# SP's transfers of a convolution loop in source order, and new start columns for the gate tiles of a ConvFFN

## The chip, the cores and the metric

The kernel runs on one core of a Trainium2 chip. The metric is the device time of one execution in microseconds (us). Engines: PE (TensorE matrix multiply; PEld is its weight load), DVE (VectorE), ACT (ScalarE), POOL (GpSimd) and SP (SyncE, which issues all the DMA transfers spoken of here).

## The reference

Two layers over 1024 latent tokens and 256 context tokens, model width 1024. Layer 0 mixes tokens with a Conformer convolution, layer 1 with windowed attention; each mixer is followed by a gated ConvFFN of inner width 2816, and each of these four steps is preceded by an RMSNorm with shift, scale and gate from an adaLN map of the conditioning vector. The two steps that the change touches (`dwconv` is a depthwise convolution, of 31 taps in the first and 3 in the second):

```python
def conformer_conv(h, w_pw1, b_pw1, w_dw, b_dw, ln_g, ln_b, w_pw2, b_pw2):
    u = h @ w_pw1 + b_pw1
    a, g = jnp.split(u, 2, axis=-1)
    v = a * jax.nn.sigmoid(g)
    v = dwconv(v, w_dw, b_dw)
    v = jax.nn.silu(layernorm(v, ln_g, ln_b))
    return v @ w_pw2 + b_pw2

def conv_ffn(h, w_up, w_dw, b_dw, w_down):
    u = dwconv(h @ w_up, w_dw, b_dw)
    a, b = jnp.split(u, 2, axis=-1)
    return (jax.nn.silu(a) * b) @ w_down
```

## The kernel before

**Layout.** Channels lie on the 128 partitions, tokens along the free axis, in three token tiles t = 0, 1, 2 of 512, 512 and 256 columns. Float32 products are made of three matrix products of rounded parts (`mm3`, matmuls at L193): each operand is split into a high part (`wh`, `x_h`, `gh`) and a remainder (`wl`, `x_l`, `gl`). Weights come by `load_raw` (L109) as 512 KB tiles `raw`, of which there are two buffers that all weights and adaLN blocks share; `split_pending` (L129, L131) makes `wh` and `wl`.

**Convolution loop (about 85 to 370 us).** It runs over 8 channel chunks c. A pass of c = 0 to 6 makes the next chunk's gated value v(c+1) with `glu_mm` (matmuls into `glu_ps`), `glu_gate` (ACT) and `glu_mul` (DVE), one token tile after the other, and convolves the chunk c: some taps on PE (`pe_taps`, `cacc`, L822), the others on DVE, ACT and POOL (`conv_steps`). PE needs shifted copies of v across partitions. So `Shifted.load(t)` stores piece t of v to DRAM (L799) and then reads it back with four `copy` transfers (L792), into `vp` for t = 0 and 1 and into `vpb` for t = 2. The copies wait until the store has landed, and that wait is SP's.

Each pass also makes one adaLN block 4 + c (`ada_steps`, matmuls into `ada_ps` at L211), of four parts of two matmuls with a 512 KB `raw` each. Parts 0 and 1 of the pass c have been fetched at the end of the pass c - 1 (`ld_ada(c, 0)` and `ld_ada(c, 1)`), parts 2 and 3 within the pass c (`ld_ada(c, 2)`, `ld_ada(c, 3)`), each after the part that frees its buffer. In the source a pass names, as far as SP is concerned:

```python
run(ada, 2)
...
ld_ada(c, 2)
ld_ada(c, 3)
...
vp.load(0)
...
w_load()
w_load()
...
vp.load(1)
...
ld_ada(c + 1, 0)
...
vp.load(2)
...
ld_ada(c + 1, 1)
```

(`run(ada, 2)` is parts 0 and 1 on PE; `w_load` fetches the next chunk's `pw1` weights.) The last pass, c = 7, has no next chunk: it convolves chunk 7 with 28 taps on PE, makes the last adaLN block, and calls `load_ada(0)` to `load_ada(3)` (L878), each a fetch of 2 MB for adaLN blocks of layer 1, which PE works on between the steps that follow the loop.

**Who orders the work.** The loop stands in a `tc.manual_schedule(engines=CONV_ENGINES)` block, in which PE, ACT, DVE and POOL issue in source order. SP is not among these engines: its order in the loop is the scheduler's, any order that the buffers and the data allow. The queue of an engine is in order, so what stands behind a waiting transfer on SP waits too.

**First ConvFFN (about 555 to 1490 us).** 22 channel groups j: two up projections (`up_ps`), three taps on ACT and DVE into a tile `c`, SiLU and product, and the split into `gh` and `gl` (`gate_steps`). After every second group the down projection (`down_half`, `down_mm`) multiplies `gh` and `gl` as moving operands by the down weights into `dn_ps`. `gh` and `gl` are tiles of the pool `fp` with three buffers each and W = 1024 + 2 + 256 = 1282 float32 columns, and a token tile is a slice of them at column 0, 512 or 1026. The last pair lies in halves of one older tile, `last_g`, whose first half starts where the tile does and the second W columns on; its products also feed `dn_tail`. The second ConvFFN has two token tiles (W = 1024) and its own pool.

Starts in the text are positions in a partition in bytes, mod 512, of a tile's first element; they follow from the order and the sizes of the tiles in the pools.

Of the kernel before, what the change touches and what calls it, by code (L numbers as in the profile page):

```python
# [8 lines left out]
F32 = mybir.dt.float32  # L9
# [9 lines left out]
P = 128  # L19
# [33 lines left out]
def hybrid_dit_kernel(  # L53
# [336 lines left out]
    def ffn(l, x_pool, fpool_stack, fpool, pas, pa, tiles, pieces, after_piece, on_half, cbufs, gbufs, extra=None, last_g=None):  # L390
        xs = list(x)
        W = SEQ + 2 + CTX if len(tiles) == 3 else SEQ
        pof = (0, 512, SEQ + 2)

        def up_ps(first=False):
# [31 lines left out]
            return c, [s0, s1, s2]  # L427

        def gate_steps(ca, cb, res, windows=((0, W),), g=None):
            gh, gl = g or [fpool.tile([P, W], F32R, tag=tag, name=tag, bufs=gbufs)  # L430
                           for tag in ("gh", "gl")]
            res.append((gh, gl))
            steps = []
            for o, e in windows:
                def s0(o=o, e=e):
                    nc.vector.tensor_mul(out=cb[:, o:e], in0=ca[:, o:e], in1=cb[:, o:e])

                def s1(o=o, e=e):
                    nc.scalar.copy(out=gh[:, o:e], in_=cb[:, o:e])
                    nc.vector.tensor_sub(out=gl[:, o:e], in0=cb[:, o:e], in1=gh[:, o:e])  # L440

                steps += [s0, s1]
            return steps
# [165 lines left out]
    with ExitStack() as cs:  # L609
# [250 lines left out]
        def ymean(c):  # L860
            for t, (o, n) in enumerate(TOK):
                nc.tensor.matmul(mean_ps[32 * t:32 * t + 32, :n], lhsT=ones2, rhs=ys[t][:, c, :],
                                 start=c == 0, stop=c == KC - 1)
# [41 lines left out]
        def ld_ada(c, u):  # L905
            if c < KC:
                araw[c, u] = load_raw(adaw[0, 4 + c, :, 2 * u:2 * u + 2, :])
# [14 lines left out]
        with tc.manual_schedule(engines=CONV_ENGINES):  # L922
            load_next(True)
            stats(0)
            ada0(2)
            bcast_a(0)
            bcast_b(0)
            normalize_h(0)
            ada0(0)
            load_next(True)  # L930
            load_block(1)
            load_h(2, nc.sync)
            w4 = load_taps()
            apply(0, 0, 2)
            stats(1, nc.vector, 0, 4)
            apply(0, 2, 4)
            split_pending()
            split_pending()
            q = glu_begin(0)
            ada0(3)  # L940
            stats(1, nc.vector, 4, 8)
            glu_mm(q, 0, 0, 0)
            stats(2, nc.vector, 0, 4)
            stats(2, nc.vector, 4, 8)
            bcast_a(1)
            ada0(1)
            bcast_a(2)
            bcast_b(1)
            apply(0, 4, 6)
            apply(0, 6, 8)  # L950
            glu_mm(q, 0, 1, 0)
            glu_mm(q, 0, 0, 1)
            normalize_h(1)
            glu_mm(q, 0, 1, 1)
            apply(1, 0, 2)
            glu_out(q, 0)
            apply(1, 2, 4)
            bcast_b(2)
            glu_mm(q, 1, 0, 0)
            normalize_h(2)  # L960
            apply(1, 4, 6)
            apply(1, 6, 8)
            apply(2, 0, 4)
            apply(2, 4, 8)
            pack_taps(w4)
            dgs = tap_weights(0)
            glu_mm(q, 1, 1, 0)
            glu_mm(q, 1, 0, 1)
            glu_mm(q, 1, 1, 1)
            w_load()  # L970
            w_load()
            vp = Shifted(0, q.v)
            vp.load(0)
            glu_out(q, 1)
            vp.load(1)
            wh = w_hi()
            glu_mm(q, 2, 0)
            w_lo(wh)
            glu_mm(q, 2, 1)
            glu_out(q, 2)  # L980
            vp.load(2)
            w_lo(w_hi())
            ys = [make_h(t, "y") for t in range(3)]

            ld_ada(0, 0)
            ld_ada(0, 1)
            fin = None
            for c in range(KC):
                wide_taps = M[c] * P > 256
                if wide_taps:  # L990
                    dgs = tap_weights(c)
                r, taps = pe_taps(c, vp, dgs)
                first, pq, dq, last = conv_steps(c, q.v, r, NPE[c], NDV[c])
                ada_ps = pc.tile([P, 512], F32, tag="s", name="ada_ps", bufs=2) if c == KC - 1 else None
                ada = ada_steps(0, 4 + c, lambda u, c=c: araw[c, u], ada_ps)
                if c + 1 < KC:
                    q = glu_begin(c + 1)
                    glu_mm(q, 0, 0)
                    glu_gate(q, 0)
                    glu_mm(q, 0, 1)  # L1000
                    glu_mul(q, 0)
# [3 lines that stand above are left out]
                    if fin:  # L1005
                        fin()
                    run(taps, 4)
                    first()
                    run(pq, 3)
                    vp = Shifted(c + 1, q.v)  # L1010
                    vp.load(0)
                    if c > 0:
                        ymean(c - 1)
# [3 lines that stand above are left out]
                    glu_mm(q, 1, 0)  # L1017
                    run(ada, 1)
                    run(pq, 2)
                    glu_gate(q, 1)  # L1020
                    run(pq, 1)
                    glu_mm(q, 1, 1)
                    run(dq, 9)
                    glu_mul(q, 1)
                    vp.load(1)
                    wh = w_hi()
                    run(pq, 1)
                    if M[c + 1] * P <= 256:
                        dgs = tap_weights(c + 1)
                    glu_mm(q, 2, 0)  # L1030
                    run(dq, 1)
                    w_lo(wh)
                    ld_ada(c + 1, 0)
                    run(pq, 1)
                    glu_gate(q, 2)
                    wh = w_hi()
                    glu_mm(q, 2, 1)
                    run(dq, 1)
                    glu_mul(q, 2)
                    vp.load(2)  # L1040
                    w_lo(wh)
                    ld_ada(c + 1, 1)
                    run(pq, 99)
                    run(dq, 99)
                    fin = ada.pop()
                else:
                    fin()
                    first()
                    run(pq, 99)
                    ymean(c - 1)  # L1050
                    run(taps, 2)
                    run(ada, 2)
                    ld_ada(c, 2)
                    ld_ada(c, 3)
                    run(taps, 2)
                    run(ada, 3)
                    for i in range(4):
                        load_ada(i)
                    run(dq, 99)
                last()  # L1060
# [256 lines left out]

    with ExitStack() as fs:
        fp = pool(fs, "fp")
        pas = fs.enter_context(ExitStack())  # L1320
        pa = pool(pas, "pa", 2, space=PSUM)

        def rest_of_ada(j):
            if j % 2 == 1 and ADA_EARLY + j // 2 < 12:
                ada_block(1, ADA_EARLY + j // 2)
            if j == NJ - 1:
                ada_mul(1, 0)
                ada_mul(1, 1)

        def norm_piece(t, o, n, acc, sqs):  # L1330
            r = {}

            def bcast():
                rb = rstd_bcast(acc, n, r["dg"])
                x[t] = make_x(xpool_of(t), t, "x10_")
                r["steps"] = norm_steps_of(hs[t], n, rb, *x[t], 1, 0, 1 if t == 2 else 0, 1, 2 if t == 2 else 2, None if t == 1 else [sqs[1][:, k] for k in range(4, 8)])

            return [(lambda: r.update(dg=rstd_diag(acc, n)), 2), bcast] + \
                [(lambda: r["steps"].pop(0)(), 1 if t == 2 else 0.85)] * (KC + 1)

        def last_g(W):
            g = xp1.tile([P, KC * 512], F32R, tag="xl1", name="last_g")
            return g[:, 0:W], g[:, W:2 * W]

        def next_weights():
            load_next(True)
            load_next(True)
            split_pending()
            clock.after(1, [lambda: split_pending(True, False)])
            clock.after(4.4, [lambda: split_pending(False, True)])  # L1350

        ffn(0, xpool_of, fs, fp, pas, pa, (0, 1, 2), ((2, 0, CTX), (0, 0, 512), (1, 0, 512)), norm_piece,
            next_weights, 2, 3, rest_of_ada, last_g)


# [477 lines left out]
```

## Time and profile before

| | |
|---|---|
| device time, median of 3 runs | 2737.51 us (2736.82 to 2739.61) |
| profiled execution | 2738.22 us, of which span 2736.4 us |
| mean granted clock of PE | 0.99 |
| busy share of PE, PEld, DVE, ACT, POOL | 96, 79, 59, 36, 20% |
| DMA | 225.38 MB, 82 GB/s over the span |
| convolution loop | about 85 to 370 us, some 36 us a pass |

The span runs from the first to the last instruction of the profiled execution, and the rest of that execution's time lies around it. Start times below are us from the start of the span. A granted clock of 1.00 means 2.4 GHz for PE and 0.50 means 1.2 GHz. In a timeline, "x8" is the number of instructions that a row takes together, and a bracket at its end gives the idle time before it and what ended that. DMA issues of SP show there with the time that issuing took; the time to landing is in the view of DMA issues and in the chain of waits.

### The profile page before, as it was taken

The page shows a single profiled execution, that of the slowest core. Times are in us where ns is not written, and L with a number is a line of the kernel's source. Part 1 is how long each engine was busy: PE and PEld are TensorE (multiplying, and loading weights), DVE is VectorE, ACT ScalarE, POOL GpSimd, SP SyncE. Part 2 cuts the span into 40 slices and gives each one's busy share as a digit, 9 for nine tenths or more (in the row PEclk, how much of TensorE's full clock was granted, in tenths as well). Part 3 has the DMA queues.
Part 4 walks back from the last instruction along what each step waited for, and adds up shares of the span by engine and source line. Part 5 has one row for each costly group of instructions (what it writes and reads, how often), then busy time and mean ns, then how long its engine had stood idle before and what let it go on. Part 6 is the DMA issues. An engine that isn't in the chain of part 4 may idle for free.

```text
span 2736.4 us, 34110 instructions
## 1 busy us (share of the span) xinstructions
PE 2635.3 (96%) x13860; PEld 2150.8 (79%) x13860; DVE 1617.1 (59%) x2273; ACT 982.9 (36%) x1396; POOL 555.3 (20%) x384
## 2 busy tenths in 40 slices
PE   5999979999999999999999998999999999999997
PEld 3777746778888888888887787888878888888886
DVE  6588634555445455445447658899854555555546
ACT  5444435542221112211124327777642222222223
POOL 1588713310000000000004106566510000000003
PEclk8999999999999999999999999999999999999998
DMA  6555763311111111111111542231111111111111
GB/s 246 172 178 180 257 238 114 136 61 48 39 40 38 39 39 39 39 39 39 39 39 51 166 160 59 60 86 48 47 54 46 47 54 47 47 46 47 54 46 70
DMA packets 81775, 225.38 MB, mean 82 GB/s; under 512 B 10833, under 2 KB 22737, under 8 KB 79313
## 3 DMA queue, kind: packets, MB, share of 16 engines
q1 hardware_dynamic: 81616, 223.20, 24.5%
q8 instruction: 109, 1.79, 0.3%
q14 instruction: 50, 0.40, 0.0%
HBM read 202.00 MB, written 21.16 MB: 82 GB/s over the span
## 4 chain that ended last, share of the span: by engine, by line
PE 81%; DVE 9%; ACT 6%; DMA 2%; issue 2%; POOL 1%; SPq 0%; DVEq 0%; ACTq 0%; POOLq 0%
PE up_ps L193 39%; PE dn_ps L193 18%; PE glu_ps L193 7%; PE wo_ps L193 2%; PE pw_ps L193 2%; PE pB L193 2%; PE pA L193 2%; PE cacc L822 2%; DVE tl L178 1%; PE tp L1544 1%; PE v_ps L193 1%; DVE mx L1522 1%; PE ada_ps L211 1%; ACT p L1526 1%; PE dn_tail L193 1%
## 5 line engine op out<-in xcount | busy, mean ns | idle before, releaser
L131 DVE TENSOR_TENSOR wl<-raw,wh 128x1024 fp32r<-128x1024 f32 x165 | 204.8, 1242 | 516.0 <-issue 312.4
L193 PE MATMUL up_ps<-x_l,wh 128*128 128x512 f32 (+1 forms) x1760 | 414.9, 370 | 4.2 <-POOL x_l L322 4.2
L193 PE MATMUL up_ps<-x_h,wl 128*128 128x512 f32 (+1 forms) x1760 | 409.7, 369 | 0.2 <-ACT x_h L311 0.2
L193 PE MATMUL up_ps<-x_h,wh 128*128 128x512 f32 (+1 forms) x1760 | 407.9, 369 | 0.0
L193 PEld LDWEIGHTS up_ps<-x_l,wh 128*128 128x128 f32 x1760 | 311.8, 189 | 64.2 <-POOL x_l L322 5.8
L257 POOL TENSOR_TENSOR acc<-acc,scrh 128x256 f32<-128x256 f32 (+1 forms) x36 | 37.5, 1040 | 1575.3 <-ACT scrh L256 1573.5
L193 PEld LDWEIGHTS up_ps<-x_h,wh 128*128 128x128 f32 x1760 | 311.3, 189 | 55.8 <-issue 0.8
L193 PEld LDWEIGHTS up_ps<-x_h,wl 128*128 128x128 f32 x1760 | 310.4, 189 | 56.2 <-issue 0.8
L461 DVE SCALAR_TENSOR_TENSOR y<-dn_ps,mods,y 128x512 f32<-128x512 f32 (+1 forms) x400 | 270.3, 694 | 128.9 <-PE dn_ps L193 128.7
L416 ACT ACTIVATE c<-up_ps,pv 128x1282 f32<-128x1282 f32 (+1 forms) x88 | 115.6, 1315 | 588.5 <-PE up_ps L193 588.5
L129 ACT CAST wh<-raw 128x1024 fp32r<-128x1024 f32 x178 | 185.5, 1043 | 357.7 <-PE dn_ps L193 328.1
L193 PE MATMUL dn_ps<-gl,wh 128*128 128x512 f32 (+1 forms) x800 | 232.9, 372 | 0.7 <-DVE y L461 0.7
L193 PE MATMUL dn_ps<-gh,wl 128*128 128x512 f32 (+1 forms) x800 | 231.5, 371 | 0.0
L193 PE MATMUL dn_ps<-gh,wh 128*128 128x512 f32 (+1 forms) x800 | 231.1, 370 | 0.0
L849 POOL TENSOR_TENSOR a<-a,pr 128x1295 f32<-128x1295 f32 x62 | 194.2, 3132 | 73.2 <-ACT pr L848 70.1
L1538 POOL TENSOR_TENSOR p<-p,rd 128x640 f32<-128x640 f32 (+1 forms) x128 | 154.7, 1240 | 232.6 <-DVE rd L1536 165.0
L420 DVE SCALAR_TENSOR_TENSOR c<-up_ps,pv,c 128x1281 f32<-128x1281 f32 (+1 forms) x88 | 124.6, 1416 | 121.7 <-ACT c L416 121.7
L193 PEld LDWEIGHTS dn_ps<-gl,wh 128*128 128x128 f32 x800 | 142.7, 188 | 31.8 <-DVE y L461 6.4
L193 PEld LDWEIGHTS dn_ps<-gh,wh 128*128 128x128 f32 x800 | 145.1, 188 | 27.0
L193 PEld LDWEIGHTS dn_ps<-gh,wl 128*128 128x128 f32 x800 | 145.0, 188 | 26.9
L843 DVE SCALAR_TENSOR_TENSOR cacc<-v,pv,cacc 128x1295 f32<-128x1295 f32 x86 | 135.0, 1569 | 31.2 <-PE cacc L822 29.0
L424 DVE SCALAR_TENSOR_TENSOR c<-up_ps,pv,c 128x1281 f32<-128x1281 f32 (+1 forms) x88 | 124.5, 1416 | 2.3
(255 smaller groups left out, 4015.1 us busy)
## 6 DMA issues: line engine op xcount, KB each, us to landing
raw<-in_up_dram SPq DMA_DIRECT2D x88, 512.0 KB, 3.4
ada<-in_adaw_dram SPq DMA_DIRECT2D x11, 2048.0 KB, 9.6
raw<-in_down_dram SPq DMA_DIRECT2D x44, 512.0 KB, 3.4
raw<-in_adaw_dram SPq DMA_DIRECT2D x38, 512.0 KB, 4.8
raw<-in_pw_dram SPq DMA_DIRECT2D x32, 512.0 KB, 4.4
vpb<-v_dram SPq DMA_DIRECT2D x32, 256.0 KB, 3.7
qs<-q_dram SPq DMA_DIRECT2D x32, 256.0 KB, 5.8
raw<-in_wo_dram SPq DMA_DIRECT2D x16, 512.0 KB, 3.5
```

The lines of the kernel that those rows point to most:

```text
L129: nc.scalar.copy(out=wh, in_=raw)
L131: lo_engine[0].tensor_sub(out=wl, in0=raw, in1=wh)
L193: nc.tensor.matmul(ps, lhsT=w, rhs=x, start=first and n == 0, stop=last and n == len(seq) - 1)
L257: (eng or nc.gpsimd).tensor_add(out=acc, in0=acc, in1=sq)
L416: nc.scalar.activation(out=c, in_=ps[:, :W], func=AF.Identity, bias=seg("fdb", l * 2 * NJ + ab * NJ + j, 1), scale=wd[1])
L420: nc.vector.scalar_tensor_tensor(out=c[:, 1:W], in0=ps[:, 0:W - 1], scalar=wd[0], in1=c[:, 1:W], op0=ALU.mult, op1=ALU.add)
L424: nc.vector.scalar_tensor_tensor(out=c[:, 0:W - 1], in0=ps[:, 1:W], scalar=wd[2], in1=c[:, 0:W - 1], op0=ALU.mult, op1=ALU.add)
L461: nc.vector.scalar_tensor_tensor(out=h, in0=ps[:, m * n:(m + 1) * n], scalar=mod(l, 5, dc, s), in1=h, op0=ALU.mult, op1=ALU.add)
L822: nc.tensor.matmul(r["acc"][32 * g:32 * g + 32, o:e], lhsT=w[:, (4 * s + g) * 32:(4 * s + g + 1) * 32], rhs=vp.rows(g, s, o, e - o), start ...
L843: nc.vector.scalar_tensor_tensor(out=acc, in0=v[:, j:j + OW], scalar=tap(j), in1=acc, op0=ALU.mult, op1=ALU.add)
L849: return lambda: nc.gpsimd.tensor_tensor(out=r["a2"], in0=r["a2"], in1=pr, op=ALU.add)
L1538: nc.gpsimd.tensor_tensor(out=it.p4[:, hh, :it.wid], in0=it.p4[:, hh, :it.wid], in1=rd[:, hh:hh + 1].to_broadcast([P, it.wid]), op=ALU.mult)
```

## The change

Three edits. The loop gets a manual block of its own that also lists SP, so that SP issues the loop's transfers in source order. In the last pass, `load_ada(0)` and `load_ada(1)` are named before the taps (behind the last copies), and `load_ada(2)` and `load_ada(3)` stay after the last parts of the adaLN block. And the tiles `gh` and `gl` of the first ConvFFN become 1344 columns wide (WG; only W of them are used), behind an unused tile of 48 columns, `shift`, at the start of their pool, with the second half of `last_g` at column 1344. By the tiles' order and sizes, `gh` then starts at 64, 320 and 64 mod 512 and `gl` at 320, 64 and 320, where before `gh` started at 384, 416 and 448 and `gl` at 480, 0 and 32. In the second ConvFFN they start at 320.

```diff
--- before.py
+++ after.py
@@ -390,6 +390,7 @@
     def ffn(l, x_pool, fpool_stack, fpool, pas, pa, tiles, pieces, after_piece, on_half, cbufs, gbufs, extra=None, last_g=None):
         xs = list(x)
         W = SEQ + 2 + CTX if len(tiles) == 3 else SEQ
+        WG = -(-W // 64) * 64
         pof = (0, 512, SEQ + 2)
 
         def up_ps(first=False):
@@ -427,7 +428,7 @@
             return c, [s0, s1, s2]
 
         def gate_steps(ca, cb, res, windows=((0, W),), g=None):
-            gh, gl = g or [fpool.tile([P, W], F32R, tag=tag, name=tag, bufs=gbufs)
+            gh, gl = g or [fpool.tile([P, WG], F32R, tag=tag, name=tag, bufs=gbufs)
                            for tag in ("gh", "gl")]
             res.append((gh, gl))
             steps = []
@@ -984,6 +985,7 @@
 
             ld_ada(0, 0)
             ld_ada(0, 1)
+        with tc.manual_schedule(engines=CONV_ENGINES | {mybir.EngineType.SP}):
             fin = None
             for c in range(KC):
                 wide_taps = M[c] * P > 256
@@ -1048,13 +1050,15 @@
                     first()
                     run(pq, 99)
                     ymean(c - 1)
+                    for i in range(2):
+                        load_ada(i)
                     run(taps, 2)
                     run(ada, 2)
                     ld_ada(c, 2)
                     ld_ada(c, 3)
                     run(taps, 2)
                     run(ada, 3)
-                    for i in range(4):
+                    for i in range(2, 4):
                         load_ada(i)
                     run(dq, 99)
                 last()
@@ -1317,6 +1321,7 @@
 
     with ExitStack() as fs:
         fp = pool(fs, "fp")
+        fp.tile([P, 48], F32, name="shift")
         pas = fs.enter_context(ExitStack())
         pa = pool(pas, "pa", 2, space=PSUM)
 
@@ -1340,7 +1345,7 @@
 
         def last_g(W):
             g = xp1.tile([P, KC * 512], F32R, tag="xl1", name="last_g")
-            return g[:, 0:W], g[:, W:2 * W]
+            return g[:, 0:W], g[:, 1344:1344 + W]
 
         def next_weights():
             load_next(True)
```

## Rows read from the trace of the kernel before

**Rows 1.** The page: busy time of PE, and the chain's share by engine.

```profile
PE 2635.3 (96%) x13860; PEld 2150.8 (79%) x13860; DVE 1617.1 (59%) x2273; ACT 982.9 (36%) x1396; POOL 555.3 (20%) x384
...
PE 81%; DVE 9%; ACT 6%; DMA 2%; issue 2%; POOL 1%; SPq 0%; DVEq 0%; ACTq 0%; POOLq 0%
```

**Rows 2.** What PE waited for: us in total, times, longest.

```profile
PE cacc L822 <- DMA vp<-v_dram: 4.7, 1, 4.7
...
PE ada_ps L211 <- DMA raw<-in_adaw_dram: 3.0, 4, 1.6
```

**Rows 3.** Table by stage: us; PE, PEld, DVE, ACT, POOL busy; clock; DMA share; GB/s.

```profile
150.00:200.00 50.00, 50.00 (x321) 39.69 (x320) 42.12 (x36) 22.19 (x21) 41.83 (x21) 1.00 0.54 175
100.72:104.10 3.38, 3.10 (x7) 1.25 (x8) 3.27 (x3) 1.13 (x2) 0.00 (x0) 0.50 0.73 214
341.00:349.88 8.88, 2.28 (x11) 0.73 (x10) 3.41 (x7) 3.99 (x3) 2.69 (x1) 1.00 1.00 393
349.90:353.30 3.40, 3.40 (x16) 2.35 (x18) 0.00 (x0) 0.00 (x0) 3.13 (x2) 0.50 0.42 151
```

**Rows 4.** Timeline of SP, end of the pass c = 0: start, us issuing.

```profile
121.43 0.38 SPq L799 DMA_DIRECT2D v_dram<-v  x1
123.02 0.33 SPq L109 DMA_DIRECT2D raw<-in_adaw_dram  x1
126.18 2.46 SPq L792 DMA_DIRECT2D vpb<-v_dram  x4
```

**Rows 5.** Timeline of SP, the same pair at the end of the last of six passes.

```profile
303.52 0.33 SPq L109 DMA_DIRECT2D raw<-in_adaw_dram  x1
305.95 2.54 SPq L792 DMA_DIRECT2D vpb<-v_dram  x4
```

**Rows 6.** Timeline of PE: adaLN parts 0 and 1, first and last of six passes.

```profile
131.21 1.07 PE L211 MATMUL ada_ps<-raw,c 128*32 128x512 f32 x8
...
311.88 1.06 PE L211 MATMUL ada_ps<-raw,c 128*32 128x512 f32 x8
```

**Rows 7.** DMA issues: count, KB each, median us from issue to landing.

```profile
raw<-in_up_dram SPq DMA_DIRECT2D x88, 512.0 KB, 3.4
...
raw<-in_adaw_dram SPq DMA_DIRECT2D x38, 512.0 KB, 4.8
...
vp<-v_dram SPq DMA_DIRECT2D x28, 256.0 KB, 4.1
...
v_dram<-v SPq DMA_DIRECT2D x16, 263.5 KB, 2.4
```

**Rows 8.** Chain of waits, convolution loop: start, us, what.

```profile
93.88 7.08 DMA raw<-in_adaw_dram
...
336.15 6.63 DMA v_dram<-v
...
342.79 6.74 DMA vp<-v_dram
...
362.19 5.56 PE cacc L822 x101
```

**Rows 9.** Timeline of PE: three gaps, each with its length and releaser.

```profile
98.36 1.05 PE L211 MATMUL ada_ps<-raw,c 128*32 128x512 f32 x4 [0.94 <-DMA raw<-in_adaw_dram]
101.00 1.92 PE L211 MATMUL ada_ps<-raw,c 128*32 128x512 f32 x4 [1.59 <-DMA raw<-in_adaw_dram]
...
349.66 11.35 PE L822 MATMUL cacc<-vp,dg 128*32 128x512 f32 x107 [4.66 <-DMA vp<-v_dram]
```

**Rows 10.** Chain of waits: down projection, first and second ConvFFN.

```profile
652.90 4.17 PE dn_ps L193 x18
...
2066.46 5.44 PE dn_ps L193 x24
```

**Rows 11.** Groups by form, PE, 600 to 1458 us: busy us, mean ns.

```profile
L193 PE MATMUL dn_ps<-gh,wh 128*128 128x512 f32 x320 | 100.1, 394 | 0.0
```

**Rows 12.** Groups by form, PE, 2011 to 2650 us (second ConvFFN).

```profile
L193 PE MATMUL dn_ps<-gh,wh 128*128 128x512 f32 x288 | 88.8, 389 | 0.0
```

## The prediction

> **What bounds the kernel now.** I read the page first: PE is busy for 2635.3 of 2736.4 us and holds 81% of the chain of waits, DMA 2% [rows 1]. So a gain must shorten PE's own work or one of PE's gaps, and any new gap is paid in full. I then asked what PE waits for: two entries belong to transfers of the convolution loop, 3.0 us of `ada_ps` waiting for `raw` and 4.7 us of `cacc` waiting for `vp` [rows 2]. Third, the table by stage: in the middle of the loop (150 to 200 us) PE is busy 50.00 of 50 us, though DMA stands at 0.54 and DVE at 42 us [rows 3]. The loop has no slack on PE. Last, SP's own timeline, because the edit reorders SP.
>
> **SP's order, before and after.** In the steady chunk the scheduler had put the second early fetch of the next adaLN block, `ld_ada(c+1,1)`, between the store of the third value piece and that store's four `vpb` copies: store at 121.43, fetch at 123.02, copies from 126.18 [rows 4]. The copies cannot go before the store has landed (121.43 to 126.18, 4.75 us), and SP stands still until then. In source order `vp.load(2)` (store and copies) is named before `ld_ada(c+1,1)`, so the fetch moves behind the wait and behind the issue of four copies (2.46 us): 126.18 + 2.46 = 128.7 instead of 123.02, 5.7 us later. The same pair in the last chunk that has it: 303.52 becomes 305.95 + 2.54 = 308.5, 5.0 later [rows 5]. There are six such pairs, with delays of 5.0 to 6.4 us.
>
> Against this, `ld_ada(c,2)` and `(c,3)` move ahead of the first store, and in the last pass the four 2 MB `load_ada` fetches move behind the last copies.
>
> **Cost of the late fetch.** PE reads part 1 in the second half of the x8 group (parts 0 and 1, eight matmuls) that starts at 131.21 in the first such pass and 311.88 in the last, 0.44 us after its start: at 131.65 and 312.32 [rows 6]. How long the fetch takes from its new place is not in the trace. The nearest row is the same transfer, 4.8 us median from issue to landing; the same 512 KB on an emptier queue takes 3.4 us; the longest one on the chain 7.08 [rows 7, 8]. At 4.8 the first lands at 128.7 + 4.8 = 133.5, PE 1.85 late; the others, worked the same way, are 3.1, 2.5, 1.65, 2.4 and 1.0 late: **12.5 us** in all. At 3.4 the six give 4.5, at 7.08 about 26. I take 4.8: what lies ahead in the queue changes from a fetch and a store to 1 MB of copies, so it is not emptier. A stall does not shrink the next, since the store's time hangs on PE's matmuls and moves with them. Behind the late fetch on SP stand `ld_ada(c+1,2)`, `(c+1,3)` (which wait for PE to free the buffers) and the first store with its copies; they become late by the same stall, and so does PE, and the copies are read a chunk later: covered.
>
> The clock adds to it. The granted clock stood at 0.50 (1.2 of 2.4 GHz) for 3.38 us after the two gaps of 0.94 and 1.59, and for 3.40 us after a gap of 4.66 [rows 3, 9]; each such stretch costs half its length, 1.7 us. The new gaps are 1.0 to 3.1 us long, so some should bring it: I take two of six, **+3.4**; ends 0 and 6 x 1.7 = 10.2.
>
> **Gains of the order.**
> First chunk: PE waits 0.94 and 1.59 for `raw(0,2)` and `(0,3)`, issued behind a 263 KB store; the second takes 7.08 us from 93.88 [rows 8, 9]. Issued as soon as the buffers are free they go about 0.9 earlier and without the store ahead (263 KB at the 393 GB/s seen at full load, 0.7 us [rows 3]). The first wait goes; the second fetch lands near 99.3 where PE wants it at 98.5, 0.8 left. So 1.7 us of waiting and, probably, the half clock: 3.4; I take **-3.0** (1.7 to 4.2) as part comes back at the next late fetch.
> Middle: 3.0 - 0.94 - 1.59 leaves 0.5 us in the other two waits [rows 2, 9]: **-0.5**.
> Last chunk: the store at 336.15 takes 6.63 us and the copies behind it 6.74, with the 2 MB fetches ahead in the queue, DMA at 1.00 and 393 GB/s; PE stands until 349.66 and runs 3.40 us at half clock [rows 3, 8, 9]. Without them the store should take its median 2.4 and the first copy 4.1 [rows 7], landing near 343, before PE has finished the mean at 345.0 (349.66 - 4.66). So the taps start 4.66 earlier, and 1.7 of half clock may go. But the next work has a new deadline: `load_ada(0)`, `(1)` now start near 348, 2 x 2.1 MB at 393 GB/s is 10.7 us, and `raw(7,2)`, `(7,3)` queue behind them and land near 364 and 365, where PE, after 11.35 us of taps less 1.7 and 5.56 more [rows 8, 9], wants them at 361 to 363. The last adaLN block then ends about 3.5 earlier, not 6.5: **-3.5** (2 to 5.5). The moved fetches themselves are covered: PE uses the first only after that block, and the others after the steps of the normalisation in between.
>
> **Gate tiles.** No instruction is added; the one multiply-accumulate stream that changes is the down projection of the first ConvFFN, whose moving operands are `gh` and `gl` (for the last pair the halves of `last_g`, the second moved to column 1344). Before, they start at 384, 416, 448, 480, 0 or 32 mod 512; in the second ConvFFN at 320. On the chain 18 `dn_ps` matmuls take 4.17 us in the first (231.9 ns each), 24 take 5.44 in the second (226.7) [rows 10]. By busy time it is 100.1/320 = 312.8 against 88.8/288 = 308.3 ns [rows 11, 12]. 960 matmuls of 512 columns (320 of each of three products) x 5.0 ns = 4.8, and 0.4 for the 64 of the tail: **-5.2**. The trace has no 512-column moving operand at 64, where half of the tiles go; the ends are -2.4 (only 320 helps) and 0 (the start does nothing). I take -5.2, because the slow starts form one stretch, from 384 over 512 to 32, and 64 lies outside it as 320 does; 64 is also the start nearest to a slow one, which is why the other ends stay in the range.
> The Trainium skill ("TensorE: Matmul & The Clock Gate", Back-to-back issue gap) gives the gap of a warm matmul from its columns alone, about 216 ns for 512; by it the start is worth nothing and the sum would be 5.2 us higher (rival 3 below). The trace speaks against it so far: 231.9 and 226.7 ns stand side by side for the same shape.
>
> **Sum.** +12.5 + 3.4 - 3.0 - 0.5 - 3.5 - 5.2 = +3.7 us on the profiled 2738.2 (span 2736.4 and 1.8 around it). That execution lies 0.7 above the median of 2737.5, so I forecast 2741.2. A measurement of this kernel can tell about 0.2%, 5.5 us, from no change: below 2732.0 is faster, above 2743.0 slower.
>
> **Rivals.**
> 1. *Faster: the fetch is in time.* If it lands in 3.4 us or less from its new place, since nothing else is queued then, the stalls are 4.5 or nothing and the clock does not fall: -12.2 to -7.7, **2725 to 2730**. For it: DMA has 0.46 free in the loop [rows 3]. Against it: PE's need comes 3 us after the new issue in most chunks, and no group of 512 KB fetches has a median below the 3.4 of [rows 7].
> 2. *Slower: the clock falls after every stall.* The place is the six x8 groups, the price 10.2 instead of 3.4, so +10.5, **2748**. It decides where the stalls are as long as the gaps that brought the half clock in [rows 9], 2.5 us in two pieces; landings longer than 4.8 lead here too.
> 3. *The gate tiles' start does nothing* (they don't come to lie there, or 231.9 ns has another reason, as three token tiles in place of two): +8.9, **2746.4**. For it: only one pair of stages shows the difference.
>
> **How the numbers follow.** Forecast 0.47 (own range 2736 to 2746: 0.34 within 0.2%, 0.13 slower); rival 1 0.22 (all faster); rival 2 0.17 (slower); rival 3 0.14 (0.10 slower, 0.04 within). So faster 0.22, same 0.38, slower 0.40. Cases of both signs hold most of it; the range goes from 2727, inside rival 1, to 2749, past rival 2.
>
> **What would show it.** Right: on SP the fetch `ld_ada(c+1,1)` directly behind the `vpb` copies, PE waits of 1 to 3 us before the middle of the x8 groups in six chunks, taps of the last chunk starting 4 to 5 us earlier against that chunk's own mean, 18 `dn_ps` matmuls in 4.08 us. Wrong: x8 groups still in 1.07 us without a wait (rival 1), granted clock below 1.00 after each (rival 2), 4.17 us unchanged (rival 3).

## The result and the profile after

The changed kernel takes **2764.30 us** (median of 5 runs, 2760.14 to 2767.85) against 2737.51: ratio 1.0095, 95% interval 1.0081 to 1.0110, so 26.8 us slower. The forecast of 2741.2 us (2727 to 2749) had the sign right and the late fetch as its largest term, but the measured time lies far outside its range. The profiled execution took 2760.14 us, with a span of 2758.4; it is the fastest of the five, 22.0 us of span over the profiled execution of before.

The page of the changed kernel, answering to [rows 1]: busy time of PE, and the chain's share by engine.

```profile
PE 2643.7 (96%) x13860; PEld 2151.0 (78%) x13860; DVE 1617.3 (59%) x2273; ACT 982.2 (36%) x1396; POOL 555.0 (20%) x384
...
PE 76%; DVE 9%; ACT 5%; DMA 4%; POOL 3%; issue 2%; SPq 1%; DVEq 0%; ACTq 0%; POOLq 0%
```

PE's busy time rose by 8.4 us although it has the same 13860 matmuls, and the chain has moved from PE (81 to 76%) to DMA (2 to 4%) and POOL. What PE waited for, answering to [rows 2]: us in total, times, longest.

```profile
PE ada_ps L211 <- DMA raw<-in_adaw_dram: 22.4, 9, 4.2
...
PE ymean L863 <- DVE y L854: 1.9, 1, 1.9
```

The wait for `vp` is gone, and the wait for `raw` has gone from 3.0 us in 4 pieces to 22.4 in 9. (The wait of 1.9 us for `y`, at the start of the last pass, was there before too.) Where the waits for `raw` come from is seen on SP, the same place as [rows 4]:

```profile
117.45 0.38 SPq L800 DMA_DIRECT2D v_dram<-v  x1
122.26 2.47 SPq L793 DMA_DIRECT2D vpb<-v_dram  x4
124.83 0.54 SPq L109 DMA_DIRECT2D raw<-in_adaw_dram  x1
```

As forecast, the fetch `ld_ada(1,1)` now stands behind the four copies: the store is issued at 117.45, SP waits 4.8 us for its landing, the copies take 2.47 us to issue, and the fetch goes at 124.83. PE's timeline, the six groups that answer to [rows 6] (of the last four only the second half), with the wait and its releaser at the end:

```profile
127.02 1.05 PE L211 MATMUL ada_ps<-raw,c 128*32 128x512 f32 x4
130.35 1.05 PE L211 MATMUL ada_ps<-raw,c 128*32 128x512 f32 x4 [2.27 <-DMA raw<-in_adaw_dram]
...
165.89 1.05 PE L211 MATMUL ada_ps<-raw,c 128*32 128x512 f32 x4
171.18 1.92 PE L211 MATMUL ada_ps<-raw,c 128*32 128x512 f32 x4 [4.24 <-DMA raw<-in_adaw_dram]
...
213.32 1.05 PE L211 MATMUL ada_ps<-raw,c 128*32 128x512 f32 x4 [2.69 <-DMA raw<-in_adaw_dram]
...
254.20 1.05 PE L211 MATMUL ada_ps<-raw,c 128*32 128x512 f32 x4 [2.64 <-DMA raw<-in_adaw_dram]
...
294.60 1.05 PE L211 MATMUL ada_ps<-raw,c 128*32 128x512 f32 x4 [2.16 <-DMA raw<-in_adaw_dram]
...
334.16 1.91 PE L211 MATMUL ada_ps<-raw,c 128*32 128x512 f32 x4 [2.75 <-DMA raw<-in_adaw_dram]
```

Two things are to be seen. There is a wait in the middle; the six are together 16.75 us. (Of the rest, 3.58 us are a wait in the last pass, shown below, and 1.62 one in the first.) And what was one group of eight matmuls in 1.07 us is two groups of four in 1.05 us each (1.92 at half clock; the trace shows each matmul of the source as two instructions): parts 0 and 1 write different 32-row pieces of the bank and used to overlap, part 1 starting 0.45 us after part 0. A wait between them costs this 1.0 us as well, six times. The chain of waits gives the fetches' time from issue to landing:

```profile
124.83 5.47 DMA raw<-in_adaw_dram
...
164.78 6.36 DMA raw<-in_adaw_dram
...
328.16 5.95 DMA raw<-in_adaw_dram
```

The six take 5.2 to 6.4 us, where the forecast had taken 4.8. The table by stage, behind some of the waits (us, busy time of PE, PEld, DVE, ACT, POOL, granted clock, DMA share, GB/s):

```profile
130.35:135.00 4.65, 4.65 (x52) 1.90 (x55) 1.39 (x2) 1.38 (x1) 4.49 (x3) 1.00 0.65 192
171.20:177.20 6.00, 6.00 (x24) 1.68 (x28) 0.72 (x2) 0.00 (x0) 3.64 (x2) 0.50 0.46 131
215.00:218.00 3.00, 3.00 (x17) 0.77 (x20) 0.51 (x2) 0.00 (x0) 2.92 (x2) 0.50 0.71 201
334.50:337.50 3.00, 3.00 (x12) 0.92 (x12) 0.32 (x2) 1.38 (x1) 1.51 (x2) 0.50 0.30 51
368.40:371.80 3.40, 3.40 (x20) 2.69 (x21) 0.00 (x0) 3.40 (x3) 0.79 (x1) 0.51 0.24 69
389.00:399.00 10.00, 7.85 (x28) 1.69 (x28) 0.53 (x4) 0.76 (x2) 0.00 (x0) 0.50 1.03 437
```

Behind the first wait the clock stays at 1.00; behind the second it is 0.50 for 6.8 us in all, and behind the third, fourth and sixth for 3.4 us each, so 17.1 us at half clock in passes 1 to 6. In the last pass it is 3.4 us at the start of the taps, as before, though their wait for `vp` is gone, and 10.2 around the last adaLN block. That pass, SP and then PE:

```profile
373.05 1.71 SPq L879 DMA_DIRECT2D ada<-in_adaw_dram  x2
380.70 0.80 SPq L109 DMA_DIRECT2D raw<-in_adaw_dram  x2
```

```profile
390.23 3.16 PE L211 MATMUL ada_ps<-raw,c 128*32 128x512 f32 x8 [3.58 <-DMA raw<-in_adaw_dram]
```

The two fetches of 2 MB now start at 373.05; `raw(7,2)` and `raw(7,3)` follow at 380.70 and land 9.5 us later and more, 3.58 us too late for PE, and the eight matmuls take 3.16 us at half clock. Last, the down projection of the first ConvFFN, from the chain and from the groups by form, answering to [rows 10] and [rows 11]:

```profile
678.02 4.11 PE dn_ps L193 x18
```

```profile
L193 PE MATMUL dn_ps<-gh,wh 128*128 128x512 f32 x320 | 98.8, 390 | 0.0
```

18 matmuls take 4.11 us in place of 4.17, and 320 take 98.8 in place of 100.1. One period of this ConvFFN, from one such chain row to the next, went from 83.28 to 82.83 us, 4.5 us in its ten.

By stages of the two profiled executions (a tap group is the taps of one pass on PE, `cacc`): the start 2.0 us shorter (the first tap group starts between 90.4 and 94.7 us in the runs of this study, whatever the kernel), first to seventh tap group of the loop 25.5 longer (220.6 to 246.1 us), the seventh to the last 4.9 shorter, from there to the first block of layer 1's adaLN 6.0 longer, the normalisation and pw2 3.2 longer (no run isolates why), the first ConvFFN 7.1 shorter (the gates, and two stretches of 3.4 us at half clock at its start that are not there this time), the rest 1.1 longer.

### The profile page after: what moved, and what is told of

It is laid out like the page before. It is cut to its first block, busy times and chain, and to the rows that moved or that the text cites. A ratio compares the mean times of both kernels' runs of the same rounds, so it can differ in the third digit from the quotient of the medians.

```text
span 2758.4 us, 34121 instructions
## 1 busy us (share of the span) xinstructions
PE 2643.7 (96%) x13860; PEld 2151.0 (78%) x13860; DVE 1617.3 (59%) x2273; ACT 982.2 (36%) x1396; POOL 555.0 (20%) x384
## 4 chain that ended last, share of the span: by engine, by line
PE 76%; DVE 9%; ACT 5%; DMA 4%; POOL 3%; issue 2%; SPq 1%; DVEq 0%; ACTq 0%; POOLq 0%
PE up_ps L193 38%; PE dn_ps L193 18%; PE wo_ps L193 3%; PE pw_ps L193 2%; DMA raw<-in_adaw_dram 2%; POOL a L850 2%; PE pB L193 2%; PE cacc L823 2%; PE glu_ps L193 2%; PE pA L193 2%; PE tp L1549 1%; DVE tl L178 1%; PE ada_ps L211 1%; DMA v_dram<-v 1%; PE v_ps L193 1%
## 5 line engine op out<-in xcount | busy, mean ns | idle before, releaser
L193 PE MATMUL dn_ps<-gl,wh 128*128 128x512 f32 (+1 forms) x800 | 231.9, 371 | 0.8 <-DVE y L462 0.8
```

What stands on the lines that cost most here:

```text
L193: nc.tensor.matmul(ps, lhsT=w, rhs=x, start=first and n == 0, stop=last and n == len(seq) - 1)
```

## The experiments

All times are medians; a ratio is that to the kernel before on the same chip, with its 95% interval.

**1 and 2. The two halves of the change, each alone.** `gates_only` is the kernel before with the edits of the gate tiles (`WG`, `shift`, the second half of `last_g`); `order_only` is the changed kernel without them.

> The kernel before with the gate tiles at 64 and 320 alone. Theory (the gate tiles give back 4.3 us in the first ConvFFN, and all of the loss is in the order of the loop's transfers): 2737.5 - 4.3 = 2733.2 us, 18 dn_ps matmuls in 4.08 us, the loop as before. Rival (the tiles' new places cost something elsewhere, so that part of the 26.8 us loss is theirs): over 2738.

> The new order of SP without the new gate tiles. Theory: the changed kernel's time plus the 4.3 us of the gate tiles, about 2768.6 us; 18 dn_ps matmuls in 4.17 us. Rival (gate tiles cost): below 2764.

Measured: gates_only 2734.29 us, ratio 0.9976 (0.9966 to 0.9985), 4.7 us under the kernel before on its chip; order_only 2766.77, ratio 1.0102 (1.0085 to 1.0118). The whole loss is the order's, and the gate tiles give what their matmuls give.

**3. One transfer moved back.** `Shifted.load` is cut into `store` and `fetch` (the copies), and:

```diff
-                    vp.load(2)
+                    vp.store(2)
                     w_lo(wh)
                     ld_ada(c + 1, 1)
+                    vp.fetch(2)
```

> The changed kernel with one transfer moved back: ld_ada(c+1,1) stands between the store of the third piece and its four copies, as it did before. Theory (this fetch, issued 5 us late, makes the six waits of 16.7 us and the half clock behind four of them, 17.1 us long, so 8.5 us): about 25 us less than the changed kernel, 2735 to 2740; no wait over 0.5 us in the middle of the parts 0 and 1 in passes 1 to 6, the wait of 3.6 us in the last pass still there. Rival (the loss is the new manual block, or ld_ada(c,2) and (c,3) ahead of the first store): at most a quarter of it comes back, over 2757.

Measured: 2732.59 us, ratio 0.9973 (0.9961 to 0.9984). Moving this one transfer brings some 32 us. PE's waits for `raw` from 85 to 345 us are down to 1.1 us, and the last pass keeps its own (the last row is from the timeline of PE):

```profile
PE ada_ps L211 <- DMA raw<-in_adaw_dram: 1.1, 3, 0.6
```

```profile
362.28 2.32 PE L211 MATMUL ada_ps<-raw,c 128*32 128x512 f32 x6 [5.49 <-DMA raw<-in_adaw_dram]
```

**4. Is the clock part of it?** `fill` gives PE something to do in the waits of passes 2 to 6:

```diff
+            if u == 1 and fill:
+                fill(r["ps"])
...
+                def dummy(ps, c=c):
+                    for n in range(4):
+                        nc.tensor.matmul(ps[64:96, :], lhsT=ones2, rhs=ys[0][:, c - 2, :],
+                                         start=True, stop=True)
```

> The changed kernel with four extra matmuls (PE multiplies 512 columns of y by the constant 1/1024 into a part of the adaLN bank that is overwritten next; their result is not used) between parts 0 and 1 of passes 2 to 6, so that PE is not idle for most of each wait. Theory (half clock follows the wait, and is about a third of the loop's loss): the waits shrink by the 1.8 us or so of the extra matmuls, the granted clock stays at 1.00 behind most of them, and the time falls by 3 to 8 us although work is added, to 2756 to 2761. Rival (the clock falls for another reason, or its cost is hidden elsewhere): the same 2764 or, with the added work, more.

Measured: 2756.88 us, ratio 1.0064 (1.0048 to 1.0080): 7.4 us less than the changed kernel, though PE does more. In the loop only one stretch of 3.4 us at half clock is left, behind the one wait over 2.2 us. But the four matmuls took 3.2 to 3.6 us, twice what I had expected, more than most of the waits, and the profiled execution's loop was as long as that of the changed kernel. So the run shows that the clock follows PE's idle time. It does not give its price, and where its 7.4 us were gained stays open.

**5 and 6. The last pass.** Both start from `fetch_early`: `early_one` names `load_ada(0)` ahead of the last taps and the other three behind `raw(7,3)`, `early_none` all four behind it.

```diff
-                    for i in range(2):
-                        load_ada(i)
+                    load_ada(0)
...
-                    for i in range(2, 4):
+                    for i in range(1, 4):
                         load_ada(i)
```

> fetch_early with load_ada(1) also moved behind raw(7,2) and raw(7,3), so that only load_ada(0) is named before the last taps. Theory (in the last pass these two 512 KB fetches stand in the queue behind two fetches of 2 MB, which makes PE's wait of 5.5 us and the 6.9 us of half clock around it): the two fetches land about 5 us earlier, the wait falls below 1 us, and the time by 5 to 9 us against fetch_early, to about 2725. Rival (the wait only moves on, to the adaLN blocks of layer 1 that now come later): 2730 or more, with a new wait of ada_b or pw_ps for ada.

> fetch_early with all four load_ada behind raw(7,2) and raw(7,3). Theory: the last pass has no wait for raw, but load_ada(0) lands some 10 us after its issue, 3 to 5 us after PE wants it for the first adaLN block of layer 1: between early_one and fetch_early, 2726 to 2730, with a wait of ada_b for ada. Rival (that block is not on the path): the same as early_one.

Measured: early_one **2724.20 us**, ratio 0.9946 (0.9933 to 0.9958), 7 to 8 us less than fetch_early and faster than both kernels of this case. SP's order at the end of the first pass, and the table by stage of passes 1 to 6:

```profile
117.38 0.38 SPq L798 DMA_DIRECT2D v_dram<-v  x1
119.51 0.33 SPq L109 DMA_DIRECT2D raw<-in_adaw_dram  x1
121.93 2.46 SPq L793 DMA_DIRECT2D vpb<-v_dram  x4
```

```profile
128.00:310.00 182.00, 181.97 (x1198) 135.25 (x1198) 144.99 (x118) 86.81 (x80) 148.06 (x66) 1.00 0.57 180
```

The fetch goes 2.1 us behind the store and 2.4 ahead of the copies, and PE is busy for 181.97 of 182 us at full clock. early_none: 2733.14 (2724.97 to 2736.51), ratio 0.9973 (0.9963 to 0.9983), where 2726 to 2730 had been expected. The wait came at the first block of layer 1, as foreseen, but the clock's price had been left out: in the profiled execution 17 us at half clock go with it (timeline of PE, then the table by stage).

```profile
363.86 2.79 PE L211 MATMUL ada_b<-ada,c 128*32 128x512 f32 x12 [3.35 <-DMA ada<-in_adaw_dram]
```

```profile
362.60:379.60 17.00, 13.94 (x46) 3.36 (x46) 3.53 (x7) 3.34 (x6) 0.00 (x0) 0.50 0.80 342
```

**7. The first pass.** `early_back` is `fetch_early` with `ld_ada(c,2)` and `ld_ada(c,3)` between the first store and its copies.

```diff
-                    ld_ada(c, 2)
-                    ld_ada(c, 3)
...
-                    vp.load(0)
+                    vp.store(0)
+                    ld_ada(c, 2)
+                    ld_ada(c, 3)
+                    vp.fetch(0)
```

> fetch_early with ld_ada(c,2) and ld_ada(c,3) moved behind the first store (where the scheduler had put them before). Theory (naming them ahead of the store is what ended the waits of the first pass): the waits of 0.9 and 1.6 us in the first pass are back, with 3.4 us of half clock, and the time is 3 to 4 us over fetch_early, about 2736. Rival (the first pass gained through the new block, not through these two): the same as fetch_early.

Measured: 2734.47 us, ratio 0.9982 (0.9973 to 0.9991), 2.5 us over fetch_early by the two ratios, though their intervals overlap. By the profiles the first pass takes 40.0 us, as in the kernel before (39.9), and 36.6 in fetch_early. The waits of 1.03 and 1.61 us are back, and the half clock behind them:

```profile
100.40:103.80 3.40, 2.98 (x7) 1.13 (x8) 3.29 (x4) 1.02 (x2) 0.00 (x0) 0.50 0.64 217
```

**8. The late fetch by itself.** `one_late` is the changed kernel with the last pass of early_one, so that between these two only `ld_ada(c+1,1)` differs.

> The changed kernel with only load_ada(0) ahead of the last taps, so that against early_one nothing differs but ld_ada(c+1,1), which stands behind the four vpb copies again. Theory (that fetch alone costs 16.7 us of waits and about 8.5 us of half clock): early_one's 2724.2 + 25 = 2749 us, six waits of 2 to 4.3 us, no wait over 1 us in the last pass. Rival (part of the loss came from the last pass together with the loop): below 2742.

Measured: 2759.91 us, ratio 1.0068 (1.0048 to 1.0087), against early_one's 0.9946: 33 us, not 25. Six waits, as in the changed kernel:

```profile
PE ada_ps L211 <- DMA raw<-in_adaw_dram: 17.3, 6, 4.6
```

By the profiles, first to seventh tap group, it is 31.8 us: 17.3 of waits, some 6 for the overlap of parts 0 and 1 that is lost six times, and the rest, some 8, is for the most part the clock's, which can be at most 10.6 (21.2 us at half, of them 3.4 in the first pass, where one_late happened to wait 1.8 us). My 25 had left out the lost overlap.

**9 to 12. Which starts are good for the gate tiles?** The unused tile ahead of them is left out (`gates_s0`) or has 16 or 32 columns; `lead0` is gates_only without a tile of 8 columns at the start of the constants, which moves all that is placed from the left, the weights too, by 32 bytes.

```diff
-        fp.tile([P, 48], F32, name="shift")
+        fp.tile([P, 16], F32, name="shift")
...
-    const.tile([P, 8], F32, name="lead")
```

> gates_only without the unused tile, so that gate tiles start at 384 and 128 mod 512 in place of 64 and 320. Matmuls at 384 should take 232 ns as before. For those at 128: if only 64 and 320 are good places (64 mod 256), 232 ns too and the first ConvFFN as long as before; if all places from 64 to 320 are good, 227 ns and about half of the gain of 4.3 us.

> gates_only with an unused tile of 16 columns in place of 48: gate tiles at 448 and 192 mod 512. If only 64 mod 256 is a good place, 231 to 233 ns at both; if the good places are every start from 192 to 320 (and 64), 227 at 192.

> gates_only with an unused tile of 32 columns: gate tiles at 0 and 256 mod 512. If only 64 mod 256 is a good place, 230 to 232 ns at both; if all from 192 to 320 are good, 227 at 256.

> gates_only without the unused tile of 8 columns that stands first in the constants: the split weights move from 64 to 32 mod 512, the gate tiles to 32 and 288, and the up projection's moving operands lie half at 288 and half at 320. If a good place is one with the weights' start (equal mod 256), matmuls at 32 and 288 take 227 ns and those at 320 about 232. If it is 64 mod 256 whatever the weights' start, those at 320 take 227 and those at 32 and 288 about 232, and the kernel is some 10 to 20 us longer.

Start to start of consecutive 512-column matmuls in these traces, medians in ns, by the bytes mod 512 at which the moving operand and the weights start (the traces show no addresses; the starts follow from the tiles):

| moving | weights | kernel | ns |
|---|---|---|---|
| 320 | 64 | all but lead0 | 227 |
| 64 | 64 | the changed kernel | 227 |
| 384, 416, 448, 480, 0, 32 | 64 | before | 230 to 234 |
| 128, 384 | 64 | gates_s0 | 232, 231 |
| 192, 448 | 64 | gates_s16 | 232, 232 |
| 256, 0 | 64 | gates_s32 | 233, 233 |
| 32, 288 | 32 | lead0, `dn_ps` | 227, 227 |
| 288 | 32 | lead0, `up_ps` | 227 |
| 320 | 32 | lead0, `up_ps`, `glu_ps`, `pA`, `pB` | 234 |

What counts is not an address but a relation: 227 ns where the moving operand starts at the weights' start, mod 256, and 230 to 234 everywhere else tried. gates_s0, gates_s16 and gates_s32 took 2738.03, 2738.07 and 2739.20 us in one run each, about the time of the kernel before. lead0 took 2752.02 us in one run, because many moving operands, placed from the other side of the memory, stayed at 320 while the weights went to 32. A time like that had been expected with the other branch; the paces at 32, 288 and 320 decide for this one. The groups by form of the up projection of the first ConvFFN, lead0 and then gates_only:

```profile
L192 PE MATMUL up_ps<-x_h,wh 128*128 128x512 f32 x664 | 168.8, 395 | 0.0
```

```profile
L193 PE MATMUL up_ps<-x_h,wh 128*128 128x512 f32 x664 | 164.5, 389 | 0.0
```

**13. Half as much to fill.** `fill_two` is one_late with two of the extra matmuls in place of four.

> one_late with two extra matmuls (as in fill, whose four took 3.2 to 3.6 us, more than most of the waits) between parts 0 and 1 of passes 2 to 6; their result is not used. They take about 1.8 us and lie wholly within waits of 2.2 to 4.6 us. Theory (the half clock follows the idle time of PE, and costs 8 to 10 us beside the waits): the waits shrink by 1.8 us each, half clock is left behind at most two of them, and the time falls from 2759.9 to 2750 to 2754. Rival (the half clock hangs on something else in the loop): 2759 or more.

Measured: 2756.15 us, ratio 1.0058 (1.0041 to 1.0075), 3 to 4 us under one_late; a smaller gain than expected, and the intervals overlap. The table by stage of passes 1 to 6, one_late and then fill_two:

```profile
128.00:345.00 217.00, 199.73 (x1212) 140.62 (x1214) 145.60 (x120) 91.27 (x83) 151.54 (x67) 0.95 0.52 162
```

```profile
128.00:342.00 214.00, 200.92 (x1255) 140.23 (x1257) 145.74 (x118) 90.27 (x83) 152.49 (x67) 0.98 0.53 164
```

The mean granted clock rises from 0.95 to 0.98, and the stretches at half clock behind the six waits shrink from 20.5 to 10.2 us. Three are left: one follows the wait of 3.1 us in pass 1, where nothing was filled in, and one each a remaining wait of 3.0 and of 2.2. From the second tap group to the seventh the loop is 4.0 us shorter (206.2 to 202.3). In that window 7.7 us at half clock are taken off, and the time that PE stands or fills between the parts is 1.1 us less. So by these two profiles the price of a stretch is some 0.4 of its length (part of it can lie in the wait itself), and the waits remain the larger part.

**14. Late, or behind the copies?** `late_one` is one_late with the fetch behind one of the four copies.

```diff
-                    vp.load(2)
+                    vp.store(2)
+                    vp.fetch(2, [0])
                     w_lo(wh)
                     ld_ada(c + 1, 1)
+                    vp.fetch(2, [1, 2, 3])
```

> one_late with ld_ada(c+1,1) behind one of the four vpb copies in place of all four: it is issued 1.9 us earlier, still behind SP's wait for the store, and with 256 KB of copies ahead of it in place of 1 MB. If its lateness alone makes the waits (landing 5.5 us after its issue, as in the changed kernel), each of the six waits shrinks by 1.9 us and some 6 us of waits are left: 2738 to 2742. If the copies ahead in the queue also delay it, it lands in 4 to 4.8 us, the waits are 0 to 1.5 us, with no half clock: 2727 to 2733.

Measured: 2728.39 us, ratio 0.9963 (0.9950 to 0.9976), some 30 us less than one_late, for three copies that change places with a fetch. SP, and the first group on PE:

```profile
120.32 0.38 SPq L798 DMA_DIRECT2D v_dram<-v  x1
125.03 0.52 SPq L793 DMA_DIRECT2D vpb<-v_dram  x1
125.60 0.59 SPq L109 DMA_DIRECT2D raw<-in_adaw_dram  x1
126.24 1.81 SPq L793 DMA_DIRECT2D vpb<-v_dram  x3
```

```profile
129.93 1.06 PE L211 MATMUL ada_ps<-raw,c 128*32 128x512 f32 x8
```

The fetch is issued 0.6 us after the store has landed and lands at 129.80, 4.2 us later; the group at 129.93 has no wait. One wait over 0.7 us is left in passes 1 to 6, 1.33 us in pass 2. The six fetches land 4.2 to 4.6 us after their issue, against 5.3 to 6.4 in one_late. So of the waits' 17.3 us some 11 were the late issue (six times 1.9), and most of the rest the 768 KB of copies that no longer stand ahead in the queue. Against early_one, which has the fetch ahead of SP's wait, late_one is 4 to 5 us longer, and the intervals overlap: it was the last three copies that cost most, not the wait for the store.

## Why the prediction was wrong, point by point

**The sum.** In the two profiles the forecast's +12.4 us from the first to the seventh tap group (12.5 + 3.4 - 3.0 - 0.5) came out as 25.5, its -3.5 for the last pass as +1.1, and its -5.2 for the gate tiles as -4.5.

**What bounds, and the new order: right.** PE has no slack in the loop, each wait of `ada_ps` came through to the end, and SP's new order is the one that was read from the source.

**Cost of the late fetch: the right mechanism, mis-sized.** The step that failed is "I take 4.8". I had written that the queue ahead is "not emptier" and still took the median of all such fetches (in its old place this one took 4.4 to 5.1); from its new place it took 5.2 to 6.4. The 12.5 us count from part 1's place in the undisturbed group, 0.44 us after its start. Counted like that, part 1 was 20.4 us late over the six passes: 5.2 of the 7.9 us between come from the longer landing, and 2.4 from fetches that were issued 2.3 us ahead of PE's need on average and not 2.7, the cause of which stays open. And the term was not complete: after such a wait part 1 no longer overlaps part 0 and ends another 0.4 us later, so that the six cost 23.0 us at full clock (the waits of 16.75 and six times 1.0).

**The clock: mis-sized.** "I take two of six, +3.4" became four of six, 17.1 us at half clock, up to 8.5 us, and five of six in order_only and in one_late. Rival 2 was the nearest, but as it took its waits from the same landing of 4.8 us it was itself too low. What PE did before the clock fell: in passes 1 to 6 of the profiled runs it had waited 2.56 to 4.63 us, or 2.17 and 2.22, and after six other waits of 1.87 to 2.27 us it went on at full clock. The rows of before [rows 9] had shown only a pair of 0.94 and 1.59, and 4.66. The other runs add a wait of 1.82 (one_late, first pass), and the 1.9 for `y` in the last pass, behind which it fell in the changed kernel, early_one and late_one, but not in the other kernels whose taps follow it at once. So the length of a wait alone does not tell. The Trainium skill ("TensorE: Matmul & The Clock Gate", HAM oscillation) tells of a matmul kernel whose waits for DMA put it at half clock in every turn of its loop. The fill runs agree that it is PE's idle time that brings it: 17.1 us at half clock in passes 1 to 6 became 3.4 in fill, and 20.5 became 10.2 in fill_two.

**The first pass: right.** -3.0 forecast; 3.4 us by the profiles of fetch_early and early_back, 2.5 by their times. In the changed kernel itself one wait of 1.62 us was left, at full clock.

**The last pass: wrong in sign.** The taps did start without their wait of 4.66 us. But the step that gave "the last adaLN block then ends about 3.5 earlier" had the new wait at some 2 us and no price for the clock: it was 3.58 us, with 10.2 us at half clock around it, and the 3.4 us at half clock at the taps' start, of which I had written "1.7 of half clock may go", stayed. So the stretch from the seventh tap group to the first block of layer 1 came out 1.1 us longer (57.0 to 58.1). early_one shows that both could have been had: it starts that block 51.3 us after the seventh tap group.

**The gate tiles: right in size, wrong in reason.** -5.2 forecast, -4.5 by the profile and -4.7 in gates_only. I had argued from a stretch of slow starts that 64 and 320 lie outside of. Runs 9 to 12 overturn that: 128, 192 and 256 lie outside of it too and are slow, and 64 and 320 are good because the weights lie at 64. That 64, where half of the tiles went, turned out as good as 320 was luck. (By the row, the 18 matmuls take 231.7 ns each, not 231.9; the sum went by 5.0 ns and stands.) The Trainium skill's rule, by which the gap follows from the columns alone ("TensorE: Matmul & The Clock Gate", Back-to-back issue gap), does not hold here: the traces show 227 ns at one kind of place and 230 to 234 at the others.

**What stays open.** The lost overlap and the half clock share the same stretches, so how the loop's loss beyond the waits divides between them is bounded, and measured only roughly, on single profiled executions. What of the equal start mod 256 makes the matmul 5 ns shorter, and whether starts closer than 32 bytes to it would be good too, was not tried.

## What to carry to other kernels

When an engine's queue is put in source order, go through the source once as that queue: each fetch with a near deadline must be named ahead of a transfer that waits for an earlier one to land, and above all ahead of the transfers it would queue behind. Price a new wait on a full engine by three things: its length, what used to overlap across the place where it falls, and the clock behind it. And before choosing an operand's place by its address, vary the place of the other operand too.

## What was not expected of the hardware

The pace of a 512-column matmul depends on where its two operands start relative to each other: 227 ns at equal starts mod 256 bytes, 230 to 234 otherwise, over nine other starts with the weights at 64 and one with them at 32. A wait of some 2 to 4 us on PE cost about one and a half times to twice its length here, where it split a group of matmuls that overlap (1.0 us) and mostly left the granted clock at 0.50 behind it (3.4 us or more): in one_late six waits of 17.3 us made some 30 of the 33 us lost. And 768 KB of copies ahead of a 512 KB fetch in the queue made 1 us or more of its landing.
